# Other buffers for the squares of q and k, for head 0's loads and for the last pooling copies, and no address pads

## The chip, the cores and the metric

The kernel runs on one core of one Trainium2 chip. The metric is the device time of one execution in microseconds (us). A core has five engines with a queue of instructions each: TensorE (PE, matmuls, with its weight loads as PEld), VectorE (DVE), ScalarE (ACT), GpSimd (POOL) and SyncE (SP, which here only issues DMAs). An engine runs its queue in order; a semaphore holds an instruction back until its inputs are there and its output buffer is free.

## The reference

One layer over 512 positions with 1024 channels, batch 1, all in float32:

```python
def block(x, ...):
    h = rms_norm(x, norm_mix)
    z = h @ w_in      # columns: pool 1024 | lru 1024 | q, k, v 3 x 1024 | 3 x 1024 branch gates
    p = pool_mixer(...)   # 4 groups of 256 channels, windows 2/4/8/16: (mean - u) @ w_pool * pool_scale
    l = rglru_mixer(...)  # width-4 conv, block-diagonal gates, associative scan over positions
    a = stick_breaking_attention(q, k, v)  # 8 heads of 128; q and k RMS-normed per head:
    #   zz = q @ k.T * scale; w = exp(log_sigmoid(zz) + sum of later log_sigmoid(-zz)), strictly causal; w @ v
    m = sum(sigmoid(gate_b) * (branch_b @ w_branch[b]) for b in range(3))
    x = x + m @ w_out
    return x + swiglu(rms_norm(x, norm_ffn))   # inner width 2816
```

## The kernel before

Channels lie on the 128 partitions and positions along the free dimension for most of the kernel. A float32 product is made as three matmuls in `float32r`: every operand is split into a rounded `hi` and a rest `lo`, and `hi*hi + hi*lo + lo*hi` is accumulated in PSUM (`mm3`, L312 to L314). For each weight block of 128 x 1024 floats, ACT makes `whi` by a copy (`split_w`, L141) and DVE makes `wlo` by a subtraction (L142). So PE, ACT and DVE work as a pipeline on weights that SP loads into `raw` (three buffers each of `raw`, `whi`, `wlo`, pool `wp`). `emit_next` makes these splits ahead of their use at a raised priority (`AHEAD`).

A scheduler of the framework orders each engine's instructions by the order of the program and by `tc.high_priority(n)`, which moves what stands under it ahead by n. Tiles with the same tag rotate through a fixed number of buffers: a new tile waits until the last reader of the tile that it replaces has finished.

The stages in order:

- The gates of branch 0 (`ps_gate`, L740) straight from the input, with 9 `warm` matmuls (L458) before them on a tile of ones; then gates of branch 1 and the recurrent branch.
- v, k and q (`VKQ`) by seven products of half-size blocks each (`tok_product`, L837). Quarters of the result are taken out of PSUM by `snap` (ACT, L850), finished by `final` (DVE, L854), and handed to `post`. For q (t = 0) `post` squares the quarter into a tile `sq` (ACT, L797) and DVE sums it into `qss`. For k (t = 1) the sums go on to `krs`, and eight ACT copies (L816) scale the rows. Each result is stored to DRAM (`qd`, L790, issued by POOL).
- The gates of branch 2, also by seven products, with outputs `gx`, `gy` per chunk `cc`.
- The mixed stage, from about 288 us. Its main line of work on PE is `pool_chunk` for the groups `POOL = (1, 0, 3, 2)` (`ps_pool`), then `branch(1, c)` with the recurrent output (`ps_br<-yHH`), then `branch(0, c)` with the pooling output. After each half chunk `tick` takes one entry from the list `abg` (attention) and one or two from `bg` (the rest). `queue_attention` fills `abg` with the tasks of the eight heads, a new head every five ticks: `load` (q, k, v blocks `at` from `qd`, L1052, on SP), `trans` (PE transposes `pq`, L1059, then `qkh`/`qkl`), `vsplit` (`vh`/`vl`), three `scores` (`z`, the sigmoids `K` and `A`, the DVE scan `E`), `wtrans` (PE transposes `pw`, L1109, then `wth`/`wtl`) and `yout` (`py`).
- A pool chunk leaves PSUM by two ACT copies `up` (`evac_u`, L983); `pool_mean` makes the windowed means on DVE (`pw`, then `up` at L997) and splits them (`p20h` by ACT, `p20l` by DVE); `pool_back` multiplies them with the pool weights (`pps`) and splits the result (`yph`, `ypl`). In names such as `p20l` the first digit is the group, the second the half.
- `merge` (L406) multiplies a branch with its gates (`g`, loaded by SP) into the four merge tiles `m` (L413), which stay until the output product.
- The seven products of branch 2, the output product, and the feed-forward layer.

PSUM in the mixed stage has three tiles for the main line (`pmm`), two for `z`, and three `aux` tiles through which `pq`, `pw`, `py` and `pps` rotate.

SBUF pools that matter here: tag `b` of `ap0` (13 buffers of 4 KB per partition) with tag `w` (8, the blocks of the seven products); the four merge tiles (`mp`, tag `m`, 4 KB each); in the mixed stage `sp` with 30 slots `s` of 2 KB and 12 slots `l` for loads, which take the place of `ap0`. The weight tiles are 1152 floats wide and hold 1024, at an offset of 16 floats (the first ones of three stages at 0, 4, 8 and 12), and a tile `pad` of 41 floats stands ahead of the others.

Of the kernel before, what the change touches and what calls it, by code (L numbers as in the profile page):

```python
# [8 lines left out]
F32 = mybir.dt.float32  # L9
F32R = mybir.dt.float32r  # L10
BF16 = mybir.dt.bfloat16
# [22 lines left out]
AHEAD = 200  # L34
PAD = 41


OFF = 16
STEPS = (0, 4, 8, 12)
NAW, NAT, NAB = 8, 8, 13  # L40
# [27 lines left out]
def layer_kernel(ctx: ExitStack, tc: tile.TileContext, x, xt, vecs, w_in, w_qkv7, w_gate7, w_pool, w_rg, w_ig,  # L68
# [6 lines left out]
    mp = ctx.enter_context(tc.tile_pool(name="mp", bufs=4))  # L75
    wp = ctx.enter_context(tc.tile_pool(name="wp", bufs=3))
    late = ctx.enter_context(ExitStack())
    hstack = ctx.enter_context(ExitStack())
# [50 lines left out]

    def weight_tiles(nh, nl, o=0):  # L130
        return [wp.tile([P, 1024 + 128], F32R, tag=tag, name=n)[:, o:o + 1024]
                for tag, n in (("whi", nh), ("wlo", nl))]

    def split_w(raw, shape, n, o=0):
        hi, lo = weight_tiles("whi" + n, "wlo" + n, o)
        if len(shape) == 3:
            hi, lo = (t.rearrange("p (a b) -> p a b", a=shape[1]) for t in (hi, lo))
        else:
            hi, lo = (t.rearrange("p (a b c) -> p a b c", a=shape[1], b=shape[2]) for t in (hi, lo))
        with tc.high_priority(60):  # L140
            act(hi, raw, AF.Copy)  # L141
            dve.tensor_tensor(lo, raw, hi.bitcast(F32), ALU.subtract)  # L142
        return hi, lo
# [58 lines left out]
    def add_seven(un, nm, i):  # L202
# [3 lines left out]
        def make(n):  # L206
# [3 lines left out]
            src = qraw[u, {"S1": "21", "S3": "11", "S4": "12"}.get(nm, nm), i]  # L210
            o = 0
            if u >= 3:
                o = goffs.pop(0) if goffs else OFF
            parts = split_w(src, [P] + list(shape), n, o)
            if nm == "11":
# [12 lines left out]
        specs.append((("seven", u, nm, i), make))  # L228

    goffs = list(STEPS)  # L230

# [28 lines left out]
    BNEXT = {"11": ("21", BY), "S1": ("11", BX), "S2": ("12", BX)}  # L260
    boffs = list(STEPS)

# [3 lines left out]
    def add_branch7(u, nm):  # L266
        def make(n):
            if nm in ("12", "22"):
                t = wp.tile([P, 2, 4, P], F32, tag="raw", name="raw" + n)
                nc.sync.dma_start(t, bsrc(u, nm))  # L270
            else:
                t = (BY if nm in ("11", "S3") else BX)[u]
            parts = split_w(t, [P, 2, 4, P], n, boffs.pop(0) if boffs else OFF)
            if nm in BNEXT:
                m, buf = BNEXT[nm]
                nc.gpsimd.dma_start(buf[u], bsrc(u, m), accum_op=ALU.add)
            return parts
        specs.append((("b7", u, nm), make))
# [53 lines left out]

    cst.tile([P, PAD], F32, tag="pad", name="pad")
    warm = cst.tile([P, S], BF16, tag="warm", name="warm")
    dve.memset(warm, 1.0)
# [108 lines left out]
    with ExitStack() as first:  # L444
# [12 lines left out]
        for i in range(WARM):  # L457
            nc.tensor.matmul(wps[:, 0, :], warm[:, 0:P], warm, start=True, stop=True)  # L458

# [333 lines left out]
        def post(t, i, j, r):  # L793
            if t < 2:
                sq = b4([2, 512], f"sq{t}{i}{j}")
                if t == 0:
# [97 lines left out]
        for cc in range(2):  # L894
            tx, ty = b4([2, S], f"gx{cc}"), b4([2, S], f"gy{cc}")
            if cc:
# [48 lines left out]
    with ExitStack() as mix:  # L945
# [34 lines left out]

        def evac_u(ps, name):
            u = slot(name)
            act(two(u), in_order(ps), AF.Copy)  # L983
            return u
# [35 lines left out]
        def pool_chunk(g):  # L1020
            pss = chan_chunk(("pool", g), hn, 1)
            us = [evac_u(pss[j], f"up{g}{j}") for j in range(2)]
            for j in range(2):
                bg.append(lambda j=j, u=us[j]: pool_mean(g, j, u))
            if g != POOL[0]:
                queue_pool_back(POOL[POOL.index(g) - 1])
# [17 lines left out]
        def head_tasks(h):  # L1044
# [4 lines left out]
            def load():  # L1049
                for t in range(3):  # L1050
                    r = slot_ld(f"at{h}{t}", (NS, HD))
                    nc.sync.dma_start(r, qd[t, g][:, hd].rearrange("(b p) c -> p b c", p=P))  # L1052
                    st["raw", t] = r
# [119 lines left out]
        def queue_attention():  # L1173
# [8 lines left out]
            for p in range(max(todo) + 1):  # L1182
                abg.append(lambda fs=todo.get(p, ()): [f() for f in fs])

        load_pool_weights(0)
        queue_attention()
        for g in POOL:
# [110 lines left out]
    with ExitStack() as ffn:  # L1298
# [114 lines left out]
        made = [0, NDIRECT]  # L1413
        offs = []

# [13 lines left out]
        def make_a(upto):  # L1429
            while made[0] < min(upto, len(steps)):  # L1430
                c, nm = steps[made[0]]
                made[0] += 1
                if (c, nm) == (NDIRECT, "11"):
                    offs.extend(STEPS)
                while made[1] < min(c + 2, DOWN):
# [5 lines left out]
        def split_a(src, n):  # L1441
            o = offs.pop(0) if offs else OFF
            h, l = (t.rearrange("p (w k c) -> p w k c", w=2, k=4)
                    for t in weight_tiles("wh" + n, "wl" + n, o))
            act(h, src, AF.Copy)  # L1445
            dve.tensor_tensor(l, src, h.bitcast(F32), ALU.subtract)  # L1446
            return h, l
# [131 lines left out]
        def make_d(upto):  # L1579
            while dmade[0] < min(upto, len(dsets)):  # L1580
                nm, n = dsets[dmade[0]]
                dmade[0] += 1
                if dmade[0] == 1:
                    offs.extend(STEPS)
                dfetch(dmade[0])
# [156 lines left out]
```

## Time and profile before

| | us |
|---|---|
| median of 3 runs | 871.59 (871.52 to 871.70) |
| the profiled execution | 872.32 |
| its span, first to last instruction | 870.5 |
| PE busy | 860.6 (99%) |
| PE weight loads busy | 790.0 (91%) |
| DVE busy | 741.1 (85%) |
| ACT busy | 523.1 (60%) |
| POOL busy | 91.2 (10%) |

The page gives busy times over the span, with waits as idle time before an instruction and what released it. A timeline row has the start, the time until the end of the last instruction in the row, the engine, the line, the operation, output and inputs, partitions x elements, how many equal ones stand in the row (`x4`), and the idle time before it if the engine had to wait. Since PE's instructions overlap, the distance from one start to the next tells more than a row's duration.

### The profile page before, as it was taken

How to read it: one execution, taken by the hardware profiler on the slowest of the kernel's cores; microseconds unless marked ns; L12 is line 12 of the kernel's file. 1: busy time of each engine (PE TensorE's matmuls, PEld its weight loads, DVE VectorE, ACT ScalarE, POOL GpSimd, SP SyncE). 2: the span in 40 equal slices, each digit the busy share in tenths (PEclk: the TensorE clock that was granted, in tenths of full speed). 3: DMA queues.
4: the chain of work that ended last, by engine and by line, in shares of the span. 5: the costliest groups of instructions: out<-in, count | busy, mean ns of one | idle time of the engine just before them, and what ended most of it. 6: DMA issues, size and time to landing. Idle time of an engine off the chain costs nothing.

```text
span 870.5 us, 14271 instructions
## 1 busy us (share of the span) xinstructions
PE 860.6 (99%) x5563; PEld 790.0 (91%) x5563; DVE 741.1 (85%) x961; ACT 523.1 (60%) x727; POOL 91.2 (10%) x130
## 2 busy tenths in 40 slices
PE   9999999999999999999999999999999999999998
PEld 7888878888899888889889998889999999999998
DVE  7899897998796599977988786699998888899974
ACT  7554989557966565565665545464555555755642
POOL 1110002232433101000001100000000000121200
PEclk9999999999999999999999999999999999999999
DMA  9586356798582886644636955345543433797913
GB/s 339 165 287 203 98 167 187 212 324 253 178 275 73 241 243 203 221 122 151 214 103 167 199 172 169 98 139 151 156 111 97 116 104 119 228 240 194 196 42 121
DMA packets 116643, 154.08 MB, mean 177 GB/s; under 512 B 8160, under 2 KB 90080, under 8 KB 116576
## 3 DMA queue, kind: packets, MB, share of 16 engines
q1 hardware_dynamic: 103904, 107.30, 38.4%
q0 software_dynamic: 12528, 45.62, 22.0%
q8 instruction: 43, 0.70, 0.3%
q10 hardware_dynamic: 144, 0.26, 0.1%
q14 instruction: 24, 0.20, 0.1%
HBM read 132.71 MB, written 18.87 MB: 174 GB/s over the span
## 4 chain that ended last, share of the span: by engine, by line
PE 84%; DVE 7%; ACT 5%; DMA 2%; issue 1%; SPq 0%; ACTq 0%; DVEq 0%
PE ps_y L321 11%; PE ps_x L321 8%; PE ps_q L837 7%; PE ps_dy L1661 6%; PE ps_dx L1661 5%; PE ps_br L312 3%; PE ps_br L313 3%; PE ps_br L314 3%; PE ps_bY L1280 2%; PE ps_gate L740 2%; PE ps_gy L321 2%; DVE wlo L142 2%; PE ps_bX L1280 2%; PE ps_gx L321 2%; PE ps_lru L312 1%; PE ps_out L312 1%
## 5 line engine op out<-in xcount | busy, mean ns | idle before, releaser
L141 ACT ACTIVATE whi<-raw 128x1024 fp32r<-128x1024 f32 x69 | 72.9, 1056 | 78.3 <-PE ps_out L313 16.1
L142 DVE TENSOR_TENSOR wlo<-raw,whi 128x1024 fp32r<-128x1024 f32 x69 | 84.3, 1221 | 24.8 <-ACT whi L141 24.3
L142 DVE TENSOR_TENSOR wlo<-qw,whi 128x1024 fp32r<-128x1024 f32 x48 | 58.4, 1220 | 16.5 <-ACT whi L141 16.3
L141 ACT ACTIVATE whi<-qw 128x1024 fp32r<-128x1024 f32 x48 | 50.6, 1054 | 28.8 <-PE ps_q L837 14.8
L1445 ACT ACTIVATE wh_S<-w_S 128x1024 fp32r<-128x1024 f32 x36 | 38.2, 1062 | 30.2 <-PE ps_y L321 18.3
L1565 POOL DMA_DIRECT2D dw<-in_w_down_dram x20 | 17.0, 864 | 306.1 <-DMA dw<-in_w_down_dram 263.8
L1446 DVE TENSOR_TENSOR wl_S<-w_S,wh_S 128x1024 fp32r<-128x1024 f32 x36 | 43.9, 1221 | 3.2 <-ACT wh_S L1445 3.2
L1445 ACT ACTIVATE wh<-w 128x1024 fp32r<-128x1024 f32 x27 | 28.6, 1060 | 29.3 <-PE ps_x L321 9.1
L1446 DVE TENSOR_TENSOR wl<-w,wh 128x1024 fp32r<-128x1024 f32 x27 | 33.0, 1221 | 8.2 <-ACT wh L1445 8.2
L1445 ACT ACTIVATE whdS<-dw 128x1024 fp32r<-128x1024 f32 x20 | 21.2, 1061 | 20.3 <-PE ps_dy L1661 11.2
L1096 DVE TENSOR_TENSOR_SCAN E<-K,ahead 128x512 f32<-128x512 f32 (+3 forms) x32 | 25.4, 814 | 3.9 <-ACT K L1092 3.9
L1446 DVE TENSOR_TENSOR wldS<-dw,whdS 128x1024 fp32r<-128x1024 f32 x20 | 24.2, 1222 | 4.9 <-ACT whdS L1445 4.9
L312 PE MATMUL ps_br<-yHH,whi 128*128 128x512 f32 x64 | 24.6, 385 | 1.4 <-ACT up L983 1.4
L312 PE MATMUL ps_lru<-HH,whi 128*128 128x512 f32 x64 | 24.6, 384 | 0.0
L312 PE MATMUL ps_br<-yph,whi 128*128 128x512 f32 x64 | 24.5, 383 | 0.0
L312 PE MATMUL ps_pool<-HH,whi 128*128 128x512 f32 x64 | 24.5, 383 | 0.0
L312 PE MATMUL ps_gate<-HH,whi 128*128 128x512 f32 x64 | 24.4, 381 | 0.0
L313 PE MATMUL ps_lru<-HL,whi 128*128 128x512 f32 x64 | 24.3, 379 | 0.0
L314 PE MATMUL ps_lru<-HH,wlo 128*128 128x512 f32 x64 | 24.3, 379 | 0.0
L313 PE MATMUL ps_gate<-HL,whi 128*128 128x512 f32 x64 | 24.3, 379 | 0.0
L314 PE MATMUL ps_gate<-HH,wlo 128*128 128x512 f32 x64 | 24.3, 379 | 0.0
L313 PE MATMUL ps_pool<-HL,whi 128*128 128x512 f32 x64 | 24.3, 379 | 0.0
(740 smaller groups left out, 3444.5 us busy)
## 6 DMA issues: line engine op xcount, KB each, us to landing
raw<-in_w_in_dram SPq DMA_DIRECT2D x31, 512.0 KB, 5.3
qw<-in_w_qkv_dram SPq DMA_DIRECT2D x24, 512.0 KB, 6.8
dw<-in_w_down_dram POOLq DMA_DIRECT2D x20, 512.0 KB, 9.2
w<-in_w_ffn_gate_dram SPq DMA_DIRECT2D x36, 256.0 KB, 3.7
w<-in_w_ffn_up_dram SPq DMA_DIRECT2D x36, 256.0 KB, 4.2
raw<-in_w_branch_dram SPq DMA_DIRECT2D x16, 512.0 KB, 3.9
qw<-in_w_qkv_dram POOLq DMA_DIRECT2D x12, 512.0 KB, 8.1
qd<-r POOLq DMA_DIRECT2D x12, 512.0 KB, 6.7
```

The costliest lines, as they stand in the source:

```text
L141: act(hi, raw, AF.Copy)
L142: dve.tensor_tensor(lo, raw, hi.bitcast(F32), ALU.subtract)
L312: nc.tensor.matmul(ps, lh, rh, start=start, stop=False, skip_group_check=skip)
L313: nc.tensor.matmul(ps, lh, rl, start=False, stop=False, skip_group_check=skip)
L314: nc.tensor.matmul(ps, ll, rh, start=False, stop=stop, skip_group_check=skip)
L321: nc.tensor.matmul(o, a_[a][:, w, k, :], il2(b_[b][:, k, :]), start=first and n == k == 0, stop=last and n == 2 and k == 3, skip_group_che ...
L837: nc.tensor.matmul(ps[:, a, :], b_[:, k, ts_], il(a_[:, kk, :]), start=first and n == k == 0, stop=n == 2 and k == 3, skip_group_check=True)
L1096: dve.tensor_tensor_scan(E[:, c0:c0 + n][:, ::-1], K[:, c0 + 1:c0 + n + 1][:, ::-1], ahead[:, S - n:][:, ::-1], 0.0, ALU.mult, ALU.add)
L1280: nc.tensor.matmul(o, ah[x_][:, w, k, :], il2(b[k][y_]), start=first_ and n == k == 0, stop=n == 2 and k == 3, skip_group_check=True)
L1445: act(h, src, AF.Copy)
L1446: dve.tensor_tensor(l, src, h.bitcast(F32), ALU.subtract)
L1661: nc.tensor.matmul(o, a_[a][:, w, k0 + k, :], il2(b_[b][:, k, :]), start=first and i == k == 0, stop=last and i == 2 and k == nk - 1, skip ...
```

## The change

1. The tile `pad`, the spare width of the weight tiles and all offsets go; `warm` has 128 columns instead of 512 and is read four times over by the same nine matmuls.
2. The eight tiles `sq` come from the four merge tiles (tag `m`) instead of tag `b`.
3. A new pool `ex` with two tiles of 2 KB holds first head 0's q and k (`at`), whose loads get a priority of 400, and later the two `up` copies of the last pool group, which get a priority of `EARLY` = 300. These four no longer take slots of `sp`.
4. The attention is queued, and head 0's loads are emitted, ahead of `load_pool_weights(0)` instead of in the first tick. The `gx` and `gy` of chunk 1 come from tag `w`.

In the scheduled order PE's instructions are the same. On SP the q and k loads of head 0 come ahead of the three `raw` loads at 285.63. On ACT one `snap` of q (at 234.34) moves ahead of `whi`, three scalings and a square; the first `up` of group 2 (349.12) moves some ten instructions ahead, behind a `qkh`, and the second moves behind `vh` and ahead of the `whi` at 345.89. On DVE the first merge `m` (359.84) moves ahead of the product `A` and the mean `up` (359.24).

```diff
@@ -32,11 +32,8 @@
 NTICK = (1, 1)
 H = S // 2
 AHEAD = 200
-PAD = 41
-
-
-OFF = 16
-STEPS = (0, 4, 8, 12)
+
+
 NAW, NAT, NAB = 8, 8, 13
 NSP = 42
 NLD = 12
@@ -74,6 +71,7 @@
     cst = ctx.enter_context(tc.tile_pool(name="cst", bufs=1))
     mp = ctx.enter_context(tc.tile_pool(name="mp", bufs=4))
     wp = ctx.enter_context(tc.tile_pool(name="wp", bufs=3))
+    ex = ctx.enter_context(tc.tile_pool(name="ex", bufs=2))
     late = ctx.enter_context(ExitStack())
     hstack = ctx.enter_context(ExitStack())
     hp = hstack.enter_context(tc.tile_pool(name="hp", bufs=1, side="right"))
@@ -127,12 +125,12 @@
         return [t[:, 0:2, :], t[:, 2:4, :]]


-    def weight_tiles(nh, nl, o=0):
-        return [wp.tile([P, 1024 + 128], F32R, tag=tag, name=n)[:, o:o + 1024]
+    def weight_tiles(nh, nl):
+        return [wp.tile([P, 1024], F32R, tag=tag, name=n)
                 for tag, n in (("whi", nh), ("wlo", nl))]

-    def split_w(raw, shape, n, o=0):
-        hi, lo = weight_tiles("whi" + n, "wlo" + n, o)
+    def split_w(raw, shape, n):
+        hi, lo = weight_tiles("whi" + n, "wlo" + n)
         if len(shape) == 3:
             hi, lo = (t.rearrange("p (a b) -> p a b", a=shape[1]) for t in (hi, lo))
         else:
@@ -208,10 +206,7 @@
                 r = qraw[u, "12", i]
                 dve.tensor_tensor(r, r, qraw[u, "S2", i], ALU.add)
             src = qraw[u, {"S1": "21", "S3": "11", "S4": "12"}.get(nm, nm), i]
-            o = 0
-            if u >= 3:
-                o = goffs.pop(0) if goffs else OFF
-            parts = split_w(src, [P] + list(shape), n, o)
+            parts = split_w(src, [P] + list(shape), n)
             if nm == "11":
                 qraw[u, "S2", i] = r = b4(list(shape), f"qs{u}{i}")
                 dve.tensor_tensor(r, qraw[u, "21", i], src, ALU.add)
@@ -226,8 +221,6 @@
                     seven_load(un + 1, {"12": ("12",), "S2": ("22",)}.get(nm, ()))
             return parts
         specs.append((("seven", u, nm, i), make))
-
-    goffs = list(STEPS)

     def add_then(f):
         specs[-1] = (specs[-1][0], lambda n, make=specs[-1][1]: (make(n), f())[0])
@@ -258,7 +251,6 @@
               (0, "S4"), (1, "S2"), (0, "22"), (1, "12"), (1, "S4"), (1, "S3"), (1, "22"))
     BY, BX = {}, {}
     BNEXT = {"11": ("21", BY), "S1": ("11", BX), "S2": ("12", BX)}
-    boffs = list(STEPS)

     def bsrc(u, nm):
         return w_br7[u, CH[nm], KH[nm]]
@@ -270,7 +262,7 @@
                 nc.sync.dma_start(t, bsrc(u, nm))
             else:
                 t = (BY if nm in ("11", "S3") else BX)[u]
-            parts = split_w(t, [P, 2, 4, P], n, boffs.pop(0) if boffs else OFF)
+            parts = split_w(t, [P, 2, 4, P], n)
             if nm in BNEXT:
                 m, buf = BNEXT[nm]
                 nc.gpsimd.dma_start(buf[u], bsrc(u, m), accum_op=ALU.add)
@@ -330,8 +322,7 @@
         return vt[:, o:o + 1]


-    cst.tile([P, PAD], F32, tag="pad", name="pad")
-    warm = cst.tile([P, S], BF16, tag="warm", name="warm")
+    warm = cst.tile([P, P], BF16, tag="warm", name="warm")
     dve.memset(warm, 1.0)
     idn = cst.tile([P, P], F32, tag="idn", name="idn")
     make_identity(nc, idn)
@@ -455,7 +446,7 @@

         wps = pb.tile([P, 2, S], F32, tag="mm", name="warm_ps")
         for i in range(WARM):
-            nc.tensor.matmul(wps[:, 0, :], warm[:, 0:P], warm, start=True, stop=True)
+            nc.tensor.matmul(wps[:, 0, :], warm, warm.unsqueeze(1).to_broadcast([P, 4, P]), start=True, stop=True)

@@ -792,7 +783,7 @@

         def post(t, i, j, r):
             if t < 2:
-                sq = b4([2, 512], f"sq{t}{i}{j}")
+                sq = mp.tile([P, 2, 512], F32, tag="m", name=f"sq{t}{i}{j}")
                 if t == 0:
                     act(sq, r, AF.Square)
                     dve.tensor_reduce(qss[:, 2 * j:2 * j + 2, 4 * i:4 * i + 4],
@@ -892,7 +883,7 @@
             nc.gpsimd.dma_start(gd2[cc, j], t)

         for cc in range(2):
-            tx, ty = b4([2, S], f"gx{cc}"), b4([2, S], f"gy{cc}")
+            tx, ty = (b4([2, S], f"g{n}{cc}", "bw"[cc]) for n in "xy")
             if cc:

                 dve.memset(pb.tile([P, 2, S], F32, tag="mm", name="skip_g")[:, 0, 0:1], 0.0)
@@ -978,9 +969,10 @@
                 dve.tensor_tensor(lo, r, hi.bitcast(F32), ALU.subtract)
                 pool_w[2 * h + g] = (hi, lo)

-        def evac_u(ps, name):
-            u = slot(name)
-            act(two(u), in_order(ps), AF.Copy)
+        def evac_u(ps, name, last):
+            u = ex.tile([P, S], F32, tag="u", name=name) if last else slot(name)
+            with tc.high_priority(EARLY if last else 0):
+                act(two(u), in_order(ps), AF.Copy)
             return u

         def pool_mean(g, j, u):
@@ -1019,7 +1011,7 @@

         def pool_chunk(g):
             pss = chan_chunk(("pool", g), hn, 1)
-            us = [evac_u(pss[j], f"up{g}{j}") for j in range(2)]
+            us = [evac_u(pss[j], f"up{g}{j}", g == POOL[3]) for j in range(2)]
             for j in range(2):
                 bg.append(lambda j=j, u=us[j]: pool_mean(g, j, u))
             if g != POOL[0]:
@@ -1048,8 +1040,10 @@

             def load():
                 for t in range(3):
-                    r = slot_ld(f"at{h}{t}", (NS, HD))
-                    nc.sync.dma_start(r, qd[t, g][:, hd].rearrange("(b p) c -> p b c", p=P))
+                    with tc.high_priority(400 if h == 0 and t < 2 else 0):
+                        r = (ex.tile([P, NS, HD], F32, tag="u", name=f"at{h}{t}") if h == 0 and t < 2
+                             else slot_ld(f"at{h}{t}", (NS, HD)))
+                        nc.sync.dma_start(r, qd[t, g][:, hd].rearrange("(b p) c -> p b c", p=P))
                     st["raw", t] = r

             def trans():
@@ -1182,8 +1176,10 @@
             for p in range(max(todo) + 1):
                 abg.append(lambda fs=todo.get(p, ()): [f() for f in fs])

+        queue_attention()
+        abg[0]()
+        abg[0] = nothing
         load_pool_weights(0)
-        queue_attention()
         for g in POOL:
             pool_chunk(g)
         queue_pool_back(POOL[3])
@@ -1411,7 +1407,6 @@
         raw = {}
         A = {}
         made = [0, NDIRECT]
-        offs = []

         def load_a(c):
             for nm in ("11", "21", "22", "12"):
@@ -1430,8 +1425,6 @@
             while made[0] < min(upto, len(steps)):
                 c, nm = steps[made[0]]
                 made[0] += 1
-                if (c, nm) == (NDIRECT, "11"):
-                    offs.extend(STEPS)
                 while made[1] < min(c + 2, DOWN):
                     load_a(made[1])
                     made[1] += 1
@@ -1439,9 +1432,8 @@
                 A[c, nm] = split_a(raw[c, nm], f"{c}_{nm}")

         def split_a(src, n):
-            o = offs.pop(0) if offs else OFF
             h, l = (t.rearrange("p (w k c) -> p w k c", w=2, k=4)
-                    for t in weight_tiles("wh" + n, "wl" + n, o))
+                    for t in weight_tiles("wh" + n, "wl" + n))
             act(h, src, AF.Copy)
             dve.tensor_tensor(l, src, h.bitcast(F32), ALU.subtract)
             return h, l
@@ -1580,8 +1572,6 @@
             while dmade[0] < min(upto, len(dsets)):
                 nm, n = dsets[dmade[0]]
                 dmade[0] += 1
-                if dmade[0] == 1:
-                    offs.extend(STEPS)
                 dfetch(dmade[0])
                 if nm in ("12", "22"):
                     t = DR.pop((nm, n))
```

## The prediction

> **What bounds the kernel now.** I read the page first, then the waits of TensorE, then the busy times by stretch.
>
> ```profile
> span 870.5 us, 14271 instructions
> PE 860.6 (99%) x5563; PEld 790.0 (91%) x5563; DVE 741.1 (85%) x961; ACT 523.1 (60%) x727; POOL 91.2 (10%) x130
> ```
>
> TensorE (PE) is busy for 99% of the span: 870.5 less 860.6 leaves 9.9 us in which it runs nothing. The order of its matmuls is the same in both kernels, and no matmul is added or removed, so the change can gain only what PE loses to waits. Those the change can touch, from the waits of PE (total, times, longest):
>
> ```profile
> PE ps_br L312 <- ACT up L983: 1.4, 1, 1.4
> PE ps_q L837 <- ACT r L850: 0.5, 1, 0.5
> PE pq L1059 <- DMA at<-qd: 0.2, 1, 0.2
> ```
>
> They belong to the pooling copies, the q product and head 0's loads. Whether a removed wait stays removed depends on who is nearly full behind it. The busy times by stretch (length, then PE, PEld, DVE, ACT, POOL):
>
> ```profile
> 296.00:345.00 49.00, 48.78 (x254) 42.96 (x253) 43.27 (x80) 26.91 (x48) 3.26 (x7) 1.00 0.80 239
> 345.00:377.00 32.00, 30.56 (x165) 26.86 (x163) 30.02 (x51) 20.44 (x37) 1.02 (x2) 1.00 0.64 195
> 377.00:431.00 54.00, 54.00 (x299) 48.63 (x300) 42.20 (x66) 33.17 (x65) 0.89 (x1) 1.00 0.54 171
> ```
>
> Between 345 and 377 us VectorE (DVE) is busy 30.02 of 32 us, and PE 30.56: the big wait lies where DVE has 2 us of air. From 377 to 431 PE never waits. So an advance still there at 377 runs on to the end, and one that DVE eats before is lost.
>
> **The start.** The smaller `warm` shortens a memset; nine warm matmuls of the same 512 columns run, now from an operand read four times over.
>
> ```profile
> 1.46 4.02 PE L458 MATMUL warm_ps<-warm 128*128 128x512 bf16 x9 [1.46 <-DVE warm L335]
> 4.61 0.72 ACT L473 ACTIVATE hu<-xt,vt 128x512 fp32r<-128x512 f32 x1 [1.82 <-DMA xt<-in_xt_dram]
> 5.38 1.62 PE L740 MATMUL ps_gate<-hu,whi 128*128 128x512 f32 x4
> 6.83 1.03 PE L740 MATMUL ps_gate<-hu,wlo 128*128 128x512 f32 x4
> ```
>
> The first real matmul (5.38) waits for `hu` (4.61 + 0.72 = 5.33), not for the warm ones, so their earlier end gains nothing; what it may do to the clock is a rival below. Four matmuls at full clock take 1.03, of which one lasts 0.38 (rows below): a distance of 0.22 from one to the next.
>
> **Squares of q and k.** The eight squares move from the rotating "b" buffers to the merge buffers, whose first merge is `m` at 359.84 (row further down), over 100 us later. No instruction is added. The new order on ScalarE (ACT) is what counts (copies to the second gate chunk's outputs, now in "w" buffers whose weights are used up by then, keep their places, and I cost them at nothing): the copy `r<-ps_q` now stands ahead of `whi`, the three scalings and the square that precede it here.
>
> ```profile
> 231.56 1.04 ACT L141 ACTIVATE whi<-qw 128x1024 fp32r<-128x1024 f32 x1
> 232.51 0.98 ACT L816 ACTIVATE r<-r,krs 128x128 f32<-128x128 f32 x3
> 233.39 1.05 ACT L797 ACTIVATE sq<-r 128x1024 f32<-128x1024 f32 x1
> 234.34 1.01 ACT L850 ACTIVATE r<-ps_q 128x1024 f32<-128x1024 f32 x1
> 346.97 1.22 DVE L142 TENSOR_TENSOR wlo<-raw,whi 128x1024 fp32r<-128x1024 f32 x1 [0.25 <-ACT whi L141]
> ```
>
> ```profile
> 234.56 0.38 PE L837 MATMUL ps_q0S<-whi,hT1l 128*128 128x512 f32 x1
> 235.40 0.48 PE L837 MATMUL ps_q<-whi,hT3h 128*128 128x512 f32 x1 [0.46 <-ACT r L850]
> ```
>
> At a distance of 0.22 the second would start at 234.78; it starts at 235.40, so 0.62 is lost. The copy comes up to 2.8 us earlier (234.34 to 231.56), so the wait goes whole. In exchange `whi` starts about 0.95 later (the copy takes 231.56 to 232.51) and ends at 233.55 instead of 232.60; with a `wlo` of 1.22 behind it (the row of a later one is shown) its weights are whole at 234.77, just when the product can begin. At this edge between nothing and the 0.62 can come back; I take 0.2, nearer to nothing because the first matmul needs `whi` alone. Kept: 0.42.
>
> **Head 0's loads.** The q and k loads get buffers of their own and are issued on SP's queue ahead of three weight loads behind which they stood.
>
> ```profile
> 253.93 0.75 POOL L790 DMA_DIRECT2D qd<-r  x1 [2.90 <-DVE r L854]
> 285.63 6.35 SPq L148 DMA_DIRECT2D raw<-in_w_in_dram  x3
> 292.14 3.55 SPq L1052 DMA_DIRECT2D at<-qd  x4
> ```
>
> ```profile
> 298.70 0.38 PE L314 MATMUL ps_pool<-HH,wlo 128*128 128x512 f32 x1
> 299.12 0.63 PE L1059 MATMUL pq<-idn,at 128*128 128x128 f32 x4
> 300.34 0.46 PE L312 MATMUL ps_pool<-HH,whi 128*128 128x512 f32 x1
> ```
>
> ```profile
> 356.99 1.03 PE L1059 MATMUL pq<-idn,at 128*128 128x128 f32 x8
> 357.78 0.46 PE L312 MATMUL ps_br<-yHH,whi 128*128 128x512 f32 x1
> ```
>
> Eight undisturbed transposes take 0.79 from start to start (356.99 to 357.78); here they take 1.22, so 0.43 is lost, and that goes. What queues behind the moved loads on SP are the three weight loads (`raw`), and DVE, ACT and PE behind those. They begin only at 285.63, while the two loads wait for stores of which the last was issued at 253.93, 32 us before; so they are through the queue before it matters, and I cost them at nothing. Without that cover a weight load is issued two `at` issues later, 1.8 us (3.55 for four). With 0.42 this makes 0.85 at 345 us.
>
> **The last pooling copies.** Both `up` copies of the last group move forward in ACT's order: the first to an earlier stretch in which ACT has room (26.91 busy of 49), the second right behind `vh` and ahead of `whi`.
>
> ```profile
> 345.37 0.62 ACT L1069 ACTIVATE vh<-at 128x512 fp32r<-128x512 f32 x1
> 345.89 1.04 ACT L141 ACTIVATE whi<-raw 128x1024 fp32r<-128x1024 f32 x1
> 349.12 1.10 ACT L983 ACTIVATE up<-ps_pool 128x512 f32<-128x512 f32 x2
> ```
>
> ```profile
> 347.97 0.38 PE L314 MATMUL ps_br<-yHH,wlo 128*128 128x512 f32 x1
> 349.79 0.48 PE L312 MATMUL ps_br<-yHH,whi 128*128 128x512 f32 x1 [1.44 <-ACT up L983]
> ```
>
> PE would go on at 348.19 and goes on at 349.79: 1.60 lost. With the second copy done by about 346.5 (345.99 and half of 1.10) this goes whole. Gross advance: 0.42 + 0.43 + 1.60 = 2.45 us.
>
> **What gives it back.** DVE is nearly full here, and it was moved forward by 0.85 only.
>
> ```profile
> 355.73 1.62 DVE L1112 TENSOR_TENSOR wtl<-pw,wth 128x512 fp32r<-128x512 f32 x3
> 359.24 0.69 DVE L997 SCALAR_TENSOR_TENSOR up<-pw,up 128x512 f32<-128x512 f32 x1
> 359.84 0.68 DVE L413 SCALAR_TENSOR_TENSOR m<-g,ps_br 128x512 f32<-128x512 f32 x1
> 360.69 0.69 DVE L942 TENSOR_TENSOR p20l<-up,p20h 128x512 fp32r<-128x512 f32 x1 [0.16 <-ACT p20h L941]
> 361.49 0.75 DVE L1063 SCALAR_TENSOR_TENSOR qkl<-pq,qg,qkh 128x512 fp32r<-128x512 f32 x1
> ```
>
> ```profile
> 362.59 0.38 PE L312 MATMUL pps<-p30h,wph 128*128 128x512 f32 x1
> ```
>
> First, the `wlo` at 346.97, in the row shown with q, waits for `whi` (0.25 idle), and `whi` now stands behind a copy of half of 1.10: DVE comes 0.5 later, and is 0.35 ahead of before instead of 0.85. Second, the `pq` transposes at 356.99 take a buffer that the first `wtl` frees: 355.73 + 0.69 (a row of that shape) = 356.42, a slack of 0.57. PE can therefore be at most 0.35 + 0.57 = 0.92 ahead here: 1.5 of the 2.45 are gone. Third, `m` now comes before `up`. Before, it filled the time in which ACT makes `p20h` from `up`; now that stands open, and `p20l` and `qkl` come 0.60 later (359.24 to 359.84): DVE is 0.25 behind before. `pps` at 362.59 takes the buffer that `qkl` frees at 361.49 + 0.75 = 362.24, slack 0.35: PE is 0.1 ahead.
>
> ```profile
> 374.64 0.75 DVE L1011 SCALAR_TENSOR_TENSOR ypl<-pps,vt,yph 128x512 fp32r<-128x512 f32 x1
> 374.90 1.26 PE L1109 MATMUL pw<-idn,A 128*128 128x128 f32 x10
> ```
>
> Last, the third group of the ten transposes begins seven tenths into them, about 375.6, in the buffer that `ypl` frees at 375.39: slack 0.2 to 0.25 against DVE's 0.25. PE leaves about 0.05 ahead, and 54 us without a wait carry that to the end. The sum: 2.45 gross, 2.4 given back.
>
> **The pads** only move addresses; the matmuls quoted take 0.38 us from weight buffers and from slots alike, which lie differently, so I cost them at nothing; neither sign is excluded.
>
> The Trainium skill, Perfetto Trace Analysis, Optimization Strategy, says to find the gaps on the most contended engine and make what they wait for come sooner. By that alone the three gaps would be worth their 2.45 us; the DVE rows say that they move.
>
> **The rivals.** (A) The gain is kept: DVE makes up its half microsecond in its 2 us of air (rows 345 to 377), or `up` does not delay `whi`. Then 872.32 - 2.45 - 0.73 = 869.1. Against it, the chain from `whi` through `wlo`, `wtl`, `qkl` has slacks of 0.57, 0.35 and 0.25 only. Chance 0.20.
>
> (B) The warm matmuls begin earlier, by some part of their 1.46 of waiting, and the clock rises before the first real one. The first four real ones take 1.45 (5.38 to 6.83), against 0.87 at four distances of 0.22. Gain 0.58: 871.5 - 0.58 = 870.9. The Trainium skill, TensorE: Matmul & The Clock Gate, What's actually happening, has the clock judged in free-running windows of 3413 ns, so that the rise varies between runs; by that, some tenths seldom change the window, which one execution's trace can't show. Chance 0.05.
>
> (C) Slower: the moved addresses slow the reading of weights. 1 ns on each of 5563 matmuls is 5.6 us: 877.1. It decides from 0.3 ns each (1.7 us). For it: every weight buffer moves at once. Against it: equal 0.38 us from buffers at different places. Chance 0.12.
>
> (D) Slower: the advance is lost and the clock rises later, since PE now idles longer between the last warm matmul and 5.38. A warm matmul takes 0.45 (4.02 over nine), 0.23 more than a distance at full clock; eight such decide (1.8), and a second cold stretch as long as the first 4 us costs 2: 873.5. Chance 0.08.
>
> **How the numbers follow.** The profiled execution took 872.32 us: its span of 870.5 and 1.82 around it; the median shown, 871.59, is 0.73 less. Forecast: 872.32 - 0.05 - 0.73 = 871.5, chance 0.55. About 0.2% (1.74 us) is what a measurement can tell from no change. Faster is A (0.20); within it are the forecast and B (0.60); slower are C and D (0.20). The range goes from A (869.1) to where C decides (871.59 + 5563 times 0.33 ns, 873.4), which takes in most of D; C's larger prices stay out. The likeliest case's own range is 870.6 to 872.1, from 0.92 ahead (the first slack alone) to the 0.5 that `up` puts on DVE arriving at PE.
>
> **What would show it.** Right: no wait of `ps_br` for `up` near 348, of `ps_q` for `r`, of `pq` for `at`; instead new waits of PE near 356 to 363 and 375 behind `wtl`, `qkl` and `ypl`, with PE's start at 377 within 0.3 us of before. Wrong: PE leaves 377 over 1 us ahead (A), matmuls of another length than 0.38 us (C), or a first real matmul followed by another count of slow ones (B, D).

## The result: slower, by 2.0 us

The changed kernel takes 873.88 us in the median of ten executions (873.09 to 875.91), the kernel before 871.88 beside it (871.32 to 872.33): a ratio of 1.0027, with a 95% interval of 1.0019 to 1.0035. That is above the range of the prediction (869.1 to 873.4), and the interval lies wholly above 1: the kernel is slower. The profiled execution took 873.09, the quickest of the ten; its page begins:

```profile
span 871.3 us, 14259 instructions
PE 860.4 (99%) x5563; PEld 789.2 (91%) x5563; DVE 740.7 (85%) x961; ACT 522.4 (60%) x727; POOL 91.0 (10%) x130
```

PE does the same work in the same time (860.4 against 860.6), so the matmuls are no slower; it stands still for longer. Four rows from the waits of PE in the changed kernel (total, times, longest):

```profile
PE ps_q L828 <- DVE wlo L140: 2.4, 5, 1.0
PE pq L1053 <- DVE wtl L1106: 1.7, 2, 1.5
PE ps_gy L313 <- ACT gx L904: 0.2, 1, 0.2
PE pps L304 <- DVE qkl L1057: 0.2, 1, 0.2
```

The three waits that the change was made against (`up`, `r`, `at`) are gone. The second and the fourth row are in the places that the prediction named. The first and the third are not in it. Before, there was no wait for `gx`, and the row for `wlo` read

```profile
PE ps_q L837 <- DVE wlo L142: 1.2, 3, 0.7
```

Where PE gets behind is seen by laying the two traces matmul against matmul. Two rows of before, then the two that answer to them after, and three more places where PE waits after:

```profile
219.45 0.38 PE L837 MATMUL ps_q<-wlo,HH 128*128 128x512 f32 x1
224.63 0.38 PE L837 MATMUL ps_q<-wlo,hT2h 128*128 128x512 f32 x1
```

```profile
219.56 0.48 PE L828 MATMUL ps_q<-wlo,HH 128*128 128x512 f32 x1 [0.16 <-DVE wlo L140]
226.03 0.48 PE L828 MATMUL ps_q<-wlo,hT2h 128*128 128x512 f32 x1 [1.03 <-DVE wlo L140]
257.71 0.38 PE L313 MATMUL ps_gy<-hT2h,whi 128*128 128x256 f32 x1 [0.24 <-ACT gx L904]
357.75 1.12 PE L1053 MATMUL pq<-idn,at 128*128 128x128 f32 x8 [1.52 <-DVE wtl L1106]
363.78 0.48 PE L304 MATMUL pps<-p30h,wph 128*128 128x512 f32 x1 [0.18 <-DVE qkl L1057]
```

PE comes to 219 us 0.22 ahead (the start, below), is 0.21 behind once it is through the first of these places and 1.51 behind after the second: 1.73 lost in two steps, both times waiting for `wlo`. From there the account, from the matmuls just ahead of each place to those just behind it, is: 0.10 more lost by 232 us, 0.69 gained at `r`, 0.50 lost at `gx`, 0.63 gained at `at`, 1.71 gained at `up`, and 1.77, 0.44 and 0.09 given back at `wtl`, `qkl` and `ypl`. PE is 1.38 behind at 380 us. (Counted so, a wait includes the 0.10 by which the matmul behind a waiting one comes later, 0.32 after it instead of 0.22.) Up to 431 us nothing is added:

```profile
345.00:377.00 32.00, 30.30 (x159) 26.36 (x157) 28.50 (x50) 19.28 (x35) 1.80 (x4) 1.00 0.62 192
377.00:431.00 54.00, 54.00 (x304) 48.56 (x303) 42.20 (x67) 32.94 (x65) 0.70 (x1) 1.00 0.53 174
```

The two profiled executions then differ by something that the change does not touch. Between 786 and 798 us, in the feed-forward layer, PE loses 0.63 us before that it does not lose after. 0.40 of this are two places at 795 and 798 us, whose `wld` come late because a copy `whd` waits for a weight load:

```profile
792.36 1.06 ACT L1445 ACTIVATE whd<-dr 128x1024 fp32r<-128x1024 f32 x1 [4.95 <-DMA dr<-in_w_down_dram]
```

In the changed kernel the same copy waits 3.81 us. Ten of the eleven traces of the experiments do not lose these 0.40 either, and most of the ten come there earlier than the kernel before. So the spans of these two executions differ by 0.8 us only (870.5 and 871.3), while the medians differ by 2.0: the profiled execution of before, 872.32, lies above its median, and that of the changed kernel below.

### The profile page after: what moved, and what is told of

Read it like the earlier page. It is cut to its first block, busy times and chain, and to the rows that moved or that the text cites. A ratio compares the mean times of both kernels' runs of the same rounds, so it can differ in the third digit from the quotient of the medians.

```text
span 871.3 us, 14259 instructions
## 1 busy us (share of the span) xinstructions
PE 860.4 (99%) x5563; PEld 789.2 (91%) x5563; DVE 740.7 (85%) x961; ACT 522.4 (60%) x727; POOL 91.0 (10%) x130
## 4 chain that ended last, share of the span: by engine, by line
PE 77%; DVE 11%; ACT 5%; DMA 3%; issue 3%; POOL 1%; POOLq 0%; DVEq 0%; ACTq 0%
PE ps_y L313 11%; PE ps_x L313 8%; PE ps_dy L1651 6%; PE ps_dx L1651 5%; DVE wlo L140 3%; PE ps_bY L1276 2%; PE ps_gate L731 2%; PE ps_q L828 2%; PE ps_br L304 2%; PE ps_br L305 2%; PE ps_br L306 2%; PE ps_gy L313 2%; PE ps_bX L1276 2%; PE ps_gx L313 2%; DMA qw<-in_w_gate_dram 1%
```

## Where the 1.73 us come from

The timeline of DVE ahead of the two late `wlo` and with them, first before and then after (rows between are left out):

```profile
206.17 1.22 DVE L217 TENSOR_TENSOR qs<-qw,qw 128x1024 f32<-128x1024 f32 x1
207.31 1.21 DVE L804 TENSOR_REDUCE ssq<-sq 128x8 f32<-128x1024 f32 x1
209.57 0.17 DVE L805 TENSOR_SCALAR ssq<-ssq 128x8 f32<-128x8 f32 x1
211.91 1.22 DVE L217 TENSOR_TENSOR qs<-qw,qw 128x1024 f32<-128x1024 f32 x1
214.18 0.16 DVE L350 TENSOR_TENSOR krs<-rsqq 128x8 f32<-128x8 f32 x1
215.46 1.22 DVE L854 TENSOR_TENSOR r<-r,ps_q 128x1024 f32<-128x1024 f32 x1
216.59 1.22 DVE L142 TENSOR_TENSOR wlo<-qw,whi 128x1024 fp32r<-128x1024 f32 x1
223.07 1.22 DVE L142 TENSOR_TENSOR wlo<-qs,whi 128x1024 fp32r<-128x1024 f32 x1
```

```profile
205.95 1.22 DVE L212 TENSOR_TENSOR qs<-qw,qw 128x1024 f32<-128x1024 f32 x1
207.36 1.22 DVE L212 TENSOR_TENSOR qs<-qw,qw 128x1024 f32<-128x1024 f32 x1 [0.19 <-DMA qw<-in_w_qkv_dram]
209.64 1.21 DVE L795 TENSOR_REDUCE ssq<-sq 128x8 f32<-128x1024 f32 x1
211.90 0.17 DVE L796 TENSOR_SCALAR ssq<-ssq 128x8 f32<-128x8 f32 x1
215.86 0.17 DVE L341 TENSOR_TENSOR krs<-rsqq 128x8 f32<-128x8 f32 x1 [1.54 <-POOL rsqq L340]
217.15 1.22 DVE L845 TENSOR_TENSOR r<-r,ps_q 128x1024 f32<-128x1024 f32 x1
218.28 1.22 DVE L140 TENSOR_TENSOR wlo<-qw,whi 128x1024 fp32r<-128x1024 f32 x1
224.76 1.22 DVE L140 TENSOR_TENSOR wlo<-qs,whi 128x1024 fp32r<-128x1024 f32 x1
```

The second addition `qs` of q's weights stands at 211.91 before and at 207.36 after, ahead of the sums of k's squares instead of behind them. Its tile is in tag `b`, the tag that the squares have left. The sums now come behind it and behind one more `wlo`, so the last step of `ssq` stands at 211.90 instead of 209.57. GpSimd works `rsqq` out of `ssq`, and the short `krs` on DVE wait for `rsqq`. These are GpSimd's rows, before and after:

```profile
209.82 1.67 POOL L349 TENSOR_TENSOR rsqq<-ssq,mhalf 128x8 f32<-128x8 f32 x1 [9.56 <-DVE ssq L805]
212.29 0.90 POOL L218 DMA_DIRECT2D qw<-in_w_qkv_dram  x1 [0.80 <-DVE wlo L142]
```

```profile
212.28 0.88 POOL L213 DMA_DIRECT2D qw<-in_w_qkv_dram  x1 [12.30 <-DVE ssq L796]
212.89 2.94 POOL L340 TENSOR_TENSOR rsqq<-ssq,mhalf 128x8 f32<-128x8 f32 x1
```

Before, `rsqq` is done at 211.49, 2.7 us ahead of `krs`, and hides under DVE's own work. After, it starts 3.1 us later, behind a DMA issue, takes 2.94 us instead of 1.67, and ends at 215.83; DVE has nothing else in front of `krs` and stands still for 1.54 us, with `r` and the `wlo` that PE needs next queued behind. With a `rsqq` of 1.67 it would have stood still for about 0.3; why this one took longer is not shown. DVE's two idle times, 0.19 in front of `qs` and 1.54 in front of `krs`, add up to 1.73, as PE's loss does; that the two agree to the hundredth is partly chance, since PE had about 0.3 us to spare ahead of the second `wlo` (ready at 224.29 before, used at 224.63).

## The experiments

Theory Q: the loss lies there, in the order of DVE. Rival U: the raised copies `up` cost more than they gain. Rival C: the addresses and the smaller `warm` cost it. In the measurements below each kernel stands beside executions of the kernel before on the same chip.

**One part undone: the squares back in tag `b`.**

```diff
-                sq = mp.tile([P, 2, 512], F32, tag="m", name=f"sq{t}{i}{j}")
+                sq = b4([2, 512], f"sq{t}{i}{j}")
```

> The changed kernel with one part undone: the squares of q and k are back in tag b; all else is as changed, so the order of DVE and ACT up to 288 us is that of before. Theory Q (the loss lies in the q stage: with the squares out of tag b the second addition qs of q is issued ahead of the sums of k's squares, and PE waits 1.7 us for wlo at 219 and 225 us): no wait of ps_q for wlo over 0.7 us, the wait for up gone, the wait of pq for wtl there, 871.4 to 872.0, no change against before. Rival U (the raised pooling copies cost more than they gain, through wlo and wtl at 345 to 377 us): 873 to 874 as in the changed kernel. Rival C (addresses and the smaller warm tile): 873 to 874 too.

Measured: 871.66 us beside 871.98, ratio 1.0000 (0.9991 to 1.0009): no change that can be told. The waits for `wlo` are 1.2 us in all, as before, and `pq` waits 1.30 for `wtl`. The rest of the change costs nothing and gains nothing that can be measured, which was the forecast for the whole. The raised copies and the new addresses are still in this kernel, so U and C fall.

**That part alone, in the kernel before.**

```diff
-                sq = b4([2, 512], f"sq{t}{i}{j}")
+                sq = mp.tile([P, 2, 512], F32, tag="m", name=f"sq{t}{i}{j}")
```

> The kernel before with one part of the change alone: the squares of q and k come from the merge tiles. Theory Q: PE loses 1.7 us to wlo at 219 and 225 us and gets 0.62 back at 235; the time is 873.0 to 874.0, slower by 1.2 to 2, and spreads over more than 1.5 us from run to run, since the moved addition stands right behind the arrival of its weights. Rivals U and C: 871.3 to 872.0, as before.

Measured: 873.39 us beside 871.98, ratio 1.0017 (1.0008 to 1.0026). PE loses 0.34 at 219 us and 1.30 at 224.63, and DVE's wait before `krs` is the same to the hundredth:

```profile
215.97 0.17 DVE L350 TENSOR_TENSOR krs<-rsqq 128x8 f32<-128x8 f32 x1 [1.54 <-POOL rsqq L349]
```

**The squares in the merge tiles, the addition held where it was.** (`marks[-1]` is the subtraction `r` of k, quarter (0, 1); the lines that note it are left out.)

```diff
-                dve.tensor_tensor(r, qraw[u, "21", i], src, ALU.add)
+                with tc.issue_after(marks[-1]) if (u, i) == (0, 1) else ExitStack():
+                    dve.tensor_tensor(r, qraw[u, "21", i], src, ALU.add)
```

> The changed kernel with the second addition qs of q queued on DVE behind the subtraction r of k (quarter 0, 1), where it stands before; the squares stay in the merge tiles, and everything else is as changed. Theory Q: the waits of ps_q for wlo shrink to under 0.7 each, the wait for r stays gone, 871.0 to 871.8, and the spread falls to about 1 us. If the merge tiles themselves (and not the order of that one addition) cost the time, it stays at 873 to 874. Rivals U and C: 873 to 874.

Measured: 871.45 us beside 871.98, ratio 0.9995 (0.9986 to 1.0004), 2.4 below the changed kernel. With this one instruction held, the others on DVE up to 225 us fall back into the order of before, and the whole loss of 1.73 goes, with the squares still in the merge tiles and the wait for `r` still gone. PE's place at 380 us, counted from its place at 13 us, is 2.2 better than in the changed kernel. The spread (870.93 to 873.22) did not fall to 1 us; that part of the expectation was wrong.

**Pads, offsets and `warm` alone, in the kernel before.**

```diff
-OFF = 16
-STEPS = (0, 4, 8, 12)
+OFF = 0
+STEPS = ()
...
-    warm = cst.tile([P, S], BF16, tag="warm", name="warm")
+    warm = cst.tile([P, P], BF16, tag="warm", name="warm")
```

> The kernel before with one part of the change alone: no pad tile, weight tiles of 1024 floats without offsets, warm of 128 columns read four times over. All instructions stand in the order of before. Theory Q and rival U: 871.4 to 872.1, at most 0.4 less than before through the start. Rival C: 873 to 874, with matmuls that are longer by 0.3 ns or more on the mean, or more half-clock matmuls at the start.

Measured: 871.96 us beside 871.98, ratio 1.0001 (0.9992 to 1.0010). The addresses cost nothing here that can be measured, and between 13 and 380 us PE moves by 0.03 against before.

**Only `krs` moved back.** This asks whether it is the early addition or the standing still behind `krs`. The additions stay early; the `krs` instructions of quarter (1, 1) are put behind the next `r` and `wlo`. The whole helper `rsqrt` is emitted later, GpSimd's `rsqq` with it. (The lines that hold it back and note `r` are left out.)

```diff
-            rsqrt(y.rearrange("p (a b) -> p a b", a=2), s_.rearrange("p (a b) -> p a b", a=2), (2, 4),
-                  f"q{t}{i}{j}")
+            with tc.issue_after(marks[-1]) if (i, j) == (1, 1) else ExitStack():
+                rsqrt(y.rearrange("p (a b) -> p a b", a=2), s_.rearrange("p (a b) -> p a b", a=2), (2, 4),
+                      f"q{t}{i}{j}")
```

> The changed kernel with both additions qs of q left early, and only the short krs instructions of k's quarter (1, 1) put on DVE behind the next r and wlo. If PE's loss is DVE standing still behind krs for GpSimd's rsqq (1.54 us), with the finished r and wlo queued behind it: DVE's idle time before krs goes, PE's waits for wlo at 219 and 225 us shrink to under 0.5 in all, and the time is 871.2 to 872.2, near the run with qs held. If the early addition itself costs it (its wait for its weights, its 1.2 us ahead of a wlo): 873 to 874, as changed.

Measured: 873.80 us beside 872.00, ratio 1.0024 (1.0015 to 1.0033), the number of the rival. But the wait had not gone; it had moved. The rows of DVE and of GpSimd in this kernel:

```profile
220.06 0.17 DVE L341 TENSOR_TENSOR krs<-rsqq 128x8 f32<-128x8 f32 x1 [0.43 <-POOL rsqq L340]
221.67 0.17 DVE L341 TENSOR_TENSOR krs<-rsqq 128x8 f32<-128x8 f32 x1 [1.45 <-POOL rsqq L340]
```

```profile
217.40 4.24 POOL L340 TENSOR_TENSOR rsqq<-ssq,mhalf 128x8 f32<-128x8 f32 x2 [2.49 <-DVE ssq L798]
```

The first `wlo` is on time (no wait at 219 us). But `rsqq` of this quarter now starts at 217.40 instead of 212.89, GpSimd makes two of them back to back, and DVE stands still 1.88 us behind them, ahead of the second `wlo`. The run could not tell the two apart; the next one does.

**The wait taken away, the order on DVE kept.** This kernel leaves out GpSimd's `pow` for the one quarter, so its k is another there; the order of DVE's instructions stays.

```diff
-        nc.gpsimd.tensor_tensor(t, ms, e, ALU.pow)
+        if sfx == "q111":
+            t = ms
+        else:
+            nc.gpsimd.tensor_tensor(t, ms, e, ALU.pow)
```

> The changed kernel with GpSimd's rsqq of k's quarter (1, 1) left out: krs of that quarter is worked out from ssq alone, so that its instructions wait for nothing on GpSimd. All other instructions and their order on DVE, ACT and PE stay as changed, both early additions qs too. Theory Q in its sharper form (PE loses what DVE stands still behind krs): DVE's idle 1.54 us before krs goes, PE's loss at 219 and 225 us falls from 1.7 to under 0.4, and the time is 871.2 to 872.2, 1.7 to 2.3 below the changed kernel. If the early additions themselves cost the time (DVE busy with them while a wlo is due): 873 to 874, as changed.

Measured: 871.68 us beside 871.94, ratio 1.0000 (0.9991 to 1.0009), 2.2 below the changed kernel. The timeline of DVE in this kernel, at the place shown above:

```profile
213.97 0.16 DVE L344 TENSOR_TENSOR krs<-ssq 128x8 f32<-128x8 f32 x1
215.25 1.21 DVE L848 TENSOR_TENSOR r<-r,ps_q 128x1024 f32<-128x1024 f32 x1
216.38 1.22 DVE L140 TENSOR_TENSOR wlo<-qw,whi 128x1024 fp32r<-128x1024 f32 x1
```

Both additions are early, DVE does not stand still at this `krs`, and `wlo` is at 216.38 instead of 218.28. PE's loss from 219 to 232 us falls from 1.83 to 0.21. What costs the time is DVE standing still behind `krs`; the early addition by itself costs 0.21 at most.

**The chain that gives the copies' gain back.** Two kernels go on from the one with `qs` held. In the first, the second `up` has a priority that puts it behind `whi`; with that the merge `m` falls behind `up` on DVE too. In the second, only `m` is moved.

```diff
-            with tc.high_priority(EARLY if last else 0):
+            with tc.high_priority((EARLY if name[-1] == "0" else 60) if last else 0):
```

> The changed kernel with qs held as before, and the second copy up of the last pool group at priority 60 instead of 300, which puts it on ACT behind whi and the merge m on DVE behind up again. By the prediction's chain (up ahead of whi puts 0.5 us on wlo, m ahead of up 0.6 on qkl): PE's wait of pq for wtl falls from 1.5 to about 1.0, PE is 1.3 to 1.6 ahead of before at 380 us instead of 0.6, and the time is 870.4 to 871.0, 0.6 to 1.0 below the run with qs held alone. If DVE has air to make up for both anyway: no change against that run, 871.2 to 871.7.

> As the run with qs held, and the merge m alone is queued on DVE behind up; the copies up stay where the change puts them. By the chain: the wait of pq for wtl stays 1.5, the later losses at 362 and 375 us (0.41 and 0.24 with qs held) fall to under 0.4 in all, PE is about 0.9 to 1.1 ahead at 380 us, and the time is 0.2 to 0.5 below the run with qs held. If m's place is harmless: no change against it.

Measured: 871.77 us (870.08 to 875.18) and 871.57 us (870.59 to 874.77) beside 872.00, ratios 0.9999 (0.9990 to 1.0009) and 0.9998 (0.9990 to 1.0007). In the medians neither is told from the run with `qs` held. The forecast of 0.6 to 1.0 less for the first did not come true. In the traces the chain is as expected in part. The first kernel's row:

```profile
354.85 1.12 PE L1058 MATMUL pq<-idn,at 128*128 128x128 f32 x8 [1.04 <-DVE wtl L1111]
```

With `up` behind `whi` the wait for `wtl` is 1.04 instead of 1.52, and PE, counted from where each is at 13 us, is 0.92 ahead of before at 380 us instead of 0.62 with `qs` held alone. With `m` alone the wait stays 1.52, as expected, and the loss at `qkl` goes, but 0.59 is lost in one step at `ypl` instead of 0.41 and 0.24 at the two. So the place of `m` moves that loss rather than making it, and the expectation was too high. That kernel also lost 0.88 at another place, on ACT:

```profile
255.82 0.38 PE L316 MATMUL ps_gy<-hT2h,whi 128*128 128x256 f32 x1 [0.62 <-ACT gx L910]
```

There the last square of q now stands ahead of `whi` and the copy `gx` on ACT and waits for `r`; before it stood behind them. In the changed kernel the same order goes with the 0.50 in the account. The rows on ACT, before and in the changed kernel:

```profile
254.77 0.58 ACT L913 ACTIVATE gx<-ps_gy 128x512 f32<-128x512 f32 x1
255.25 1.05 ACT L797 ACTIVATE sq<-r 128x1024 f32<-128x1024 f32 x1
```

```profile
255.17 1.06 ACT L788 ACTIVATE sq<-r 128x1024 f32<-128x1024 f32 x1 [1.89 <-DVE r L845]
256.14 1.05 ACT L139 ACTIVATE whi<-qw 128x1024 fp32r<-128x1024 f32 x1
257.09 0.57 ACT L904 ACTIVATE gx<-ps_gy 128x512 f32<-128x512 f32 x1
```

**The version without these losses.** The kernel with `qs` held and `up` behind `whi`, and the last square of q back in tag `b`:

```diff
-                sq = mp.tile([P, 2, 512], F32, tag="m", name=f"sq{t}{i}{j}")
+                nm_ = f"sq{t}{i}{j}"
+                sq = (b4([2, 512], nm_) if (t, i, j) == (0, 1, 0)
+                      else mp.tile([P, 2, 512], F32, tag="m", name=nm_))
```

> The run with qs held and the second up behind whi, and the last square of q alone back in tag b, which puts it on ACT behind the first copy gx again as before. By the trace of the run with m held (PE waited 0.6 us for gx behind that square, in others 0.2 to 0.3): no wait of ps_gy for gx, the span of a quick execution 867.8 to 868.6, the median 870.2 to 871.4, below the kernel before by 0.6 to 1.8. If what spreads the times of the run with the second up behind whi lies elsewhere: a spread of over 3 us and a median near 871.8 again.

Measured: 870.41 us (869.93 to 872.90) beside 871.94, ratio 0.9987 (0.9978 to 0.9995): 1.5 us below the kernel before and 3.5 below the changed one. Nothing waits for `gx`, and PE, counted from 13 us, is 1.15 ahead of before at 380 us, 0.23 more than without the last edit. The medians of the two lie 1.4 apart; the rest of that is not explained. The profiled execution happened to be the one of 872.90, and it shows one source of spread: its first matmuls, and after them those of one further execution of the kernel without the last square's edit.

```profile
5.66 2.08 PE L734 MATMUL ps_gate<-hu,whi 128*128 128x512 f32 x4 [0.58 <-ACT hu L467]
7.53 1.91 PE L734 MATMUL ps_gate<-hu,wlo 128*128 128x512 f32 x4
```

```profile
5.53 1.13 PE L734 MATMUL ps_gate<-hu,whi 128*128 128x512 f32 x4 [0.68 <-ACT hu L467]
6.50 1.03 PE L734 MATMUL ps_gate<-hu,wlo 128*128 128x512 f32 x4
```

> One more look at the run with the second up behind whi, whose times went from 870.1 to 875.2. If the spread comes from a load that arrives later in some executions, a slower execution shows one more wait of PE, of 1 us or more, at a place where the quick one (870.08) has none; if this one is quick again, its waits are those of before within 0.2 us each.

> One more look at the changed kernel, whose times went from 873.1 to 875.9. The waits of ps_q for wlo near 219 and 225 us come again with 1.5 to 1.9 us in all if they follow from the order on DVE; if they came from a late load in that one execution, they differ by over 0.5 us.

The further execution of the kernel with `up` behind `whi` took 870.58, with the waits of the first within 0.2 us each but for 0.68 at the start, for `hu`, where the first had 0.10. It was a quick one again, so what made the slow ones slow stays open. The further execution of the changed kernel took 872.26; PE loses 0.15 at 219 us in it instead of 0.43, and 1.29 at 224.63 instead of 1.30. The order makes this second loss; the first changes from one execution to the next.

## Why the prediction was wrong

- **Squares of q and k.** This step failed. It said that no instruction is added and that the order on ACT is what counts, and so it put the order on DVE at nothing. It did not ask what else uses tag `b`: the additions `qs`, which the scheduler could then place earlier on DVE, ahead of a chain DVE, GpSimd, DVE. On ACT it followed one `snap`, and not the last square, which moved ahead of `whi` and `gx`. The list of moved instructions under "The change" lacks both. Kept was to be 0.42. Measured are 0.69 gained at `r`, with nothing lost right behind it, so the 0.2 taken off there did not come; and 1.73, 0.10 and 0.50 lost where the prediction had no term. With the one addition held, the median falls by 2.4, to 871.45.
- **Head 0's loads.** 0.43 forecast, 0.63 measured: the forecast counted the time within the eight transposes, and the first of them also began 0.20 late. Their place on SP cost PE nothing up to 345 us.
- **The last pooling copies.** 1.60 forecast, 1.71 measured, of which 0.10 is the matmul behind the wait.
- **What gives it back.** Right in its places, and right in its largest size: a wait of 1.5 for `wtl` was forecast and 1.52 is there; with `up` behind `whi` it is 1.04, so the first link is shown. `qkl` took 0.44 where 0.8 was forecast, and `ypl` 0.09 where 0.05 was. The third link, `m` ahead of `up`, was overrated: with `m` behind `up` again PE loses nearly as much, at `ypl`.
- **The sum.** 2.45 gained and 2.4 given back were forecast. In the trace 3.03 are gained, 2.30 given back, and 2.33 lost where the prediction had no term (1.73, 0.10 and 0.50): PE loses 1.60 from 13 to 380 us. With the addition held, PE keeps 0.62 there instead of the forecast 0.05. That this kernel's 871.45 lies so near the forecast 871.5 is within what medians can tell, and no proof of the sum.
- **The pads.** Cost nothing that can be measured, as taken; rival C is out by the run with the pads alone.
- **The start.** Rival B came in part: in the changed kernel's trace the first four real matmuls take 0.97 to the next, against 1.45 before, and PE is 0.22 ahead at 13 us. The late rise of rival D came in the execution of 872.90: there the matmuls come 0.43 apart up to 9.24 us and 0.22 apart after it, which leaves PE 1.7 us behind the other execution shown at 14 us. D's reason, a longer idle time ahead of the first real matmul, is not shown: the two waited 0.58 and 0.68. The Trainium skill, TensorE: Matmul & The Clock Gate, What's actually happening, says that the point of the rise varies by 500 ns either way because the windows are free-running. These two traces agree that it varies, but by more: the matmuls of the one are at the short distance from 5.85 us at the latest, those of the other from 9.24.
- **Rival A**, the gain kept, is out: the trace shows the wait for `wtl`. The Trainium skill, Perfetto Trace Analysis, Optimization Strategy, says to find the gaps on the engine that one optimizes for and to make what they wait for start sooner or finish faster. Here the three gaps were filled, and 2.30 of the 3.03 came back as waits for DVE, which was nearly as full.

## What to carry to other kernels

A tile that leaves a shared tag also moves everything that stays in it: list every user of the tag, and follow each on every engine's queue. The dangerous instruction is a short one that waits for a slow helper engine in the middle of a full queue; here a `krs` of 0.17 us held up two operations of 1.2 us each. And a wait of PE removed in a stretch where another engine is 94% busy (DVE, 30.02 of 32 us) is worth little until that engine's own chain is shortened there: with `qs` held 0.62 us stayed, and 0.92 with `up` behind `whi` too. In the medians only the version that also had the last square back could be told from the kernel before.

## What the runs showed of the hardware

A `pow` over 128 x 8 elements took GpSimd 1.67 us before, and 2.94 after, with a DMA issue just ahead of it in its queue; others in the same two traces took 2.49 to 2.62 without one, so what sets its time is not shown. The start moves the whole kernel by up to 1.9 us between executions: four first matmuls took 2.08 us in one and 1.13 in another of almost the same kernel, 0.43 and 0.22 from one to the next, which is a clock that rises later. This is as large as most of what the change does, so that the medians alone would not have shown the chain; the traces, laid matmul against matmul, did.
